# One encoder trunk on one core: bursts of small products, diagonal copies and early products put in another order

## The chip, the core and the metric

The kernel runs on one core of one Trainium2 chip. A core has a matrix engine (TensorE, PE in the profile, with its weight loads as PEld), three engines for element-wise work (VectorE or DVE, ScalarE or ACT, GpSimd or POOL) and a sync engine (SP) that mostly issues DMA transfers; ACT and POOL issue transfers too. Each engine runs its own instructions in its own order and waits on semaphores for the others. The metric is the device time of one execution in microseconds (us); a kernel's time is the median of its runs.

## The reference

The reference is a two-layer encoder over 1,024 tokens of width 1,024, with 16 learned tokens put in front (1,040 rows). Each layer:

```python
h = h + hybrid_mixer(rmsnorm(h, norm1_w[l]), w_in[l], conv_qkv_w[l], ...)
h = h + swiglu(rmsnorm(h, norm2_w[l]), w_gate_up[l], w_down[l])
```

The mixer projects to queries, keys and values of 4 heads of 128 channels, to gates, and to three inputs of a short convolution. Keys and queries are convolved and brought to unit length, and a gated delta rule is run over the sequence in both directions, in chunks. For each chunk and head it solves with a unit triangular matrix made from the products of the chunk's keys:

```python
M = jnp.where(strict, jnp.einsum('bnhid,bnhjd->bnhij', kb, k) * decay_mat, 0.0)
A = M + jnp.eye(CHUNK, dtype=M.dtype)
u = lax.linalg.triangular_solve(A, vb, left_side=True, lower=True, unit_diagonal=True)
```

The result is normalised, gated, joined with the convolution's output and projected back. The feed-forward part is `(silu(gate) * up) @ w_down` with 2,816 hidden channels. A last normalisation ends it.

## The kernel before

**Layout and precision.** Activations lie transposed: channels on the 128 partitions, the 1,040 positions along the free dimension, cut into three pieces of 346 to 348 columns (two of 512 in the second layer's last stages). Every dense product is made of three: an operand is split into a high part (a rounded copy made on ACT) and a low part (the remainder, made on DVE), and high x high, high x low and low x high are summed in PSUM (`dense`, L142, with its matmuls at L153 to L155, and `prod`, L1056, with L1061 to L1063). Each weight block is loaded by DMA, split by `wsplit` (ACT L126 for the high part, DVE L127 for the low one) or by `w_op` (L1043, L1044), and used by three matmuls per 128 rows of the contraction. Matmuls in plain float32, as the small ones below, leave two records each in the trace.

**Order.** The engines' order is not written out by hand. The program is traced in its order, each instruction carries a priority (`at_prio`, `low`), and a list scheduler with a simulated timeline orders every engine's instructions before the kernel runs. The function `after(ins, prev)` adds a dependency by hand. Work beside the dense products is put into three queues, `jobs`, `jobs2` and `jobs3`; after every piece of a dense product `dense` takes one entry off each (`None` is an empty turn). That way chunk work is spread over the projections.

**First layer's sums.** `first_sums` (L267) squares the eight input tiles, half on ACT and half on DVE, and sums each over the partitions with four 128x32 matmuls (L265), four column groups side by side.

**Chunk work.** With nine chunks of 128 positions (the first has 16), `chunk_p(c)` (L464) multiplies the chunk's keys with themselves (four matmuls, L474, in a PSUM bank "b" of two), fetches the decays, makes the exponentials (ACT L480) and writes the triangular matrices `Pv` of both directions (DVE L483). `k_out(c)` (L439) transposes the chunk's keys on PE (four transpositions, L445, in the one bank "a"), copies them on ACT (L447) and stores them. Before, `k_out` goes through `jobs` and `chunk_p` through `jobs2`, and both come up in the same pieces.

**Inverting the triangular matrices.** A 128x128 matrix is cut into 32x32 blocks. `sub_start` (L524) copies the diagonal blocks of each direction with four ACT copies (L535), turns them with a 32x32 transposition on DVE (L537) and loads unit matrices; `substitute(d)` (L540) then inverts the diagonal blocks on DVE, direction 0 first and direction 1 afterwards. `invert(d)` (L551) joins the blocks on PE: `first` (32x32 products, L574), `second_third` (32x32, L587 and L588) and five calls of `fourth_fifth` (64x64, L607 and L609) through `jobs3`. There are 32 matrices per direction (eight chunks times four heads), so `first` makes 64 small products and `second_third` 96, in two halves of 16 matrices each, with a PSUM bank for each half. Each call of `fourth_fifth` takes eight matrices; the fourth product of one group of eight runs beside the fifth of the group before it.

**Early products.** The feed-forward part uses a scheme with seven products of half matrices in place of eight. Its first four row blocks begin with two products each, made while the output projection still runs: `early_part(f, q)` (L1087) loads a weight block, splits it and calls `prod` for each bank (two in the first layer, one in the second).

Of the kernel before, what the change touches and what calls it, by code (L numbers as in the profile page):

```python
# [15 lines left out]
KT = 8  # L16
# [26 lines left out]
def trunk(ctx: ExitStack, tc: tile.TileContext, xT, w_in, w_ba, w_out, w_gu, w_dn,  # L43
# [12 lines left out]
    def big(tag, dt=F32):  # L56
        return sb.tile([128, 4, L], dt, tag=tag, name=nm(tag))
# [56 lines left out]
    mmp = [None]  # L114
    evp = [None]
    jobs, jobs2, jobs3 = [], [], []
    whi_done = [None]
    lov = [False]

    def wsplit(src, hi, lo, raw=None):  # L120

        kk = src.shape[1]
        if raw is None:
            raw = wp.tile([128, WK, 128], F32, tag="raw", bufs=2, name=nm("raw"))
        dma(raw[:, 0:kk, :], src)
        whi_done[0] = act(out=hi, in_=raw[:, 0:kk, :], func=AF.Copy)  # L126
        tt(out=lo, in0=raw[:, 0:kk, :], in1=hi.bitcast(F32), op=ALU.subtract)  # L127

    def wload(src, nk):

# [127 lines left out]

    def square(i, m):
        if m < 4:  # L260
            act(out=sqs[i], in_=hv[m], func=AF.Square)
        else:
            tt(out=sqs[i], in0=hv[m], in1=hv[m], op=ALU.mult)
        for j in range(4):
            mm(fps[32 * j:32 * j + 32, 0:260], ones[:, 0:32], sqs[i][:, 260 * j:260 * j + 260], start=(i == 0), stop=(i == KT - 1), skip_group_check=True)  # L265
# [30 lines left out]
    for l in range(DEPTH):  # L296
# [139 lines left out]
                qdma(bc, rnd[r + h].partition_broadcast(128))  # L436
                tt(out=dst[:, h, :], in0=dst[:, h, :], in1=bc, op=ALU.mult)

        def k_out(c):  # L439

            n = 16 if c == 0 else 128
            s0 = 0 if c == 0 else 16 + 128 * (c - 1)
            ps = pa()
            for h in range(H):
                nc.tensor.transpose(ps[0:n, h * 128:(h + 1) * 128], KTt[:, h, s0:s0 + n], ident)  # L445
# [18 lines left out]
        def chunk_p(c):  # L464
# [6 lines left out]
            n, s0 = span(c)  # L471
            kk = bank("b").rearrange("p (h i) -> p h i", h=4)
            for h in range(H):
                mm(kk[0:n, h, 0:n], KTt[:, h, s0:s0 + n], KTt[:, h, s0:s0 + n], start=True, stop=True)  # L474
# [46 lines left out]
        subs = {}  # L521
        Tm = None

        def sub_start():  # L524

            nonlocal Tm
            tmp0.append(big(Y[0][2]))
            Tm = sb.tile([128, 2, 128], F32, tag="off", name=nm("Tm")).rearrange("p a b -> p (a b)")
            v = [tmp0[0][:, i, 0:1024] for i in range(4)]
            for d in range(2):  # L530
                W, Xi = (v[0], v[2]) if d == 0 else [c4k("x")[:, 0:1024] for _ in range(2)]
                W, Xi, dg = (t.rearrange("p (a b) -> p a b", a=32) for t in (W, Xi, v[3 - 2 * d]))
                dma(Xi, eye_d)
                for b in range(4):
                    act(out=dg[B[b]], in_=Pv[d][B[b], :, B[b]], func=AF.Copy)  # L535

                nc.vector.transpose(out=W, in_=dg.rearrange("p q i -> p i q"))  # L537
                subs[d] = W, Xi

        def substitute(d):  # L540
            W, Xi = subs[d]
# [9 lines left out]
        def invert(d):  # L551
# [24 lines left out]
                    for (f, s) in pairs:  # L576
                        act(out=QS[B[s], qs, :], in_=ps[B[s]], func=AF.Copy, scale=-1.0)

            def second_third():
                f0, s0 = pairs[0]  # L580
                fo, so = 32 * (f0 % 2), 32 * (s0 % 2)
                for qs in halves:
                    ps = fb(32)

                    def turn(q):
                        for (f, s) in pairs:
                            mm(ps[B[f], q - qs.start, :], QS[B[s], q, :], P_[B[s], q, B[s]], start=True, stop=True, skip_group_check=True)  # L587
                        mm(ps[B[s0], q - qs.start, :], P_[B[s0], q, B[s0]], QS[B[s0], q, :], start=True, stop=True, skip_group_check=True)  # L588

                    low(lambda: [turn(q) for q in range(qs.start, qs.stop)])  # L590
                    for (f, s) in pairs:
                        act(out=P_[B[f], qs, B[s]], in_=ps[B[f]], func=AF.Copy)
                    act(out=X64[B[s0], qs, fo:fo + 32], in_=ps[B[s0]], func=AF.Copy)
                    nc.vector.tensor_copy(X64[B[f0], qs, fo:fo + 32], XB[B[f0], qs, :])
                    nc.vector.tensor_copy(X64[B[s0], qs, so:so + 32], XB[B[s0], qs, :])
                    nc.vector.memset(X64[B[f0], qs, so:so + 32], 0.0)


            F_, S_ = (slice(0, 64), slice(64, 128)) if d == 0 else (slice(64, 128), slice(0, 64))

            def fourth_fifth(q4, q5):

                ps = fb(64)

                def turn(q):
                    if q4 is not None:
                        mm(ps[S_, q, :], P_[F_, 8 * q4 + q, S_], X64[F_, 8 * q4 + q, :], start=True, stop=True, skip_group_check=True)  # L607
                    if q5 is not None:
                        mm(ps[F_, q, :], X64[S_, 8 * q5 + q, :], P_[S_, 8 * q5 + q, S_], start=True, stop=True, skip_group_check=True)  # L609

                low(lambda: [turn(q) for q in range(8)])
                if q4 is not None:
                    act(out=X64[S_, 8 * q4:8 * q4 + 8, :], in_=ps[S_], func=AF.Copy, scale=-1.0)
                if q5 is not None:
                    act(out=P_[F_, 8 * q5:8 * q5 + 8, S_], in_=ps[F_], func=AF.Copy)
# [437 lines left out]
        CW = E if E * 4 > 1024 else NB  # L1053
        NJ = NB // CW

        def prod(ps, w, t, j, first, stop=True):  # L1056
            nk = w[0].shape[1]
            for k in range(nk):
                cs = slice(CW * j, CW * j + CW)
                th, tl = (t[0][k], t[1][k]) if isinstance(t[0], list) else (t[0][:, k, :], t[1][:, k, :])  # L1060
                mm(ps[:, :CW], w[0][:, k, :], th[:, cs], start=first and k == 0, stop=False, skip_group_check=True)  # L1061
                mm(ps[:, :CW], w[0][:, k, :], tl[:, cs], start=False, stop=False, skip_group_check=True)  # L1062
                mm(ps[:, :CW], w[1][:, k, :], th[:, cs], start=False, stop=stop and k == nk - 1, skip_group_check=True)  # L1063

        def raw4(tag):
            if tag == "raw":
# [16 lines left out]

        NE = 4
        early, bks0 = {}, {}

        def early_part(f, q):  # L1087

# [536 lines left out]
```

## Time and profile before

| what | value |
|---|---|
| median of 3 runs | 2476.99 us |
| lowest and highest run | 2471.99 and 2478.96 us |
| the profiled execution | 2479.11 us |
| its span, first to last instruction | 2477.3 us |
| mean granted TensorE clock | 0.996 |
| DMA traffic | 335.26 MB, 135 GB/s |
| chain that ended last | PE 90%, DVE 4%, DMA 3%, ACT 2% |

The profile is of one execution. "Busy" is the time in which an engine's instructions were under way. Matmuls overlap in the pipeline and their ends are modelled, so a row's duration is longer than the distance to the next start; where distances matter, starts are compared. A timeline row gives the start and the length in us, the engine, the line, the operation, output and inputs, the shape and the count of merged instructions, and in brackets the idle time before it and who ended it. 32\*32, 64\*64 and 128\*32 are the rows and columns of the array that a matmul uses. The granted clock is TensorE's share of full speed.

### The profile page before, as it was taken

How to read it: one execution, taken by the hardware profiler on the slowest of the kernel's cores; microseconds unless marked ns; L12 is line 12 of the kernel's file. 1: busy time of each engine (PE TensorE's matmuls, PEld its weight loads, DVE VectorE, ACT ScalarE, POOL GpSimd, SP SyncE). 2: the span in 40 equal slices, each digit the busy share in tenths (PEclk: the TensorE clock that was granted, in tenths of full speed). 3: DMA queues.
4: the chain of work that ended last, by engine and by line, in shares of the span. 5: the costliest groups of instructions: out<-in, count | busy, mean ns of one | idle time of the engine just before them, and what ended most of it. 6: DMA issues, size and time to landing. Idle time of an engine off the chain costs nothing.

```text
span 2477.3 us, 44868 instructions
## 1 busy us (share of the span) xinstructions
PE 2450.6 (99%) x17530; PEld 2255.6 (91%) x17530; DVE 1778.2 (72%) x3296; ACT 1054.9 (43%) x1964; POOL 67.3 (3%) x157
## 2 busy tenths in 40 slices
PE   9999999999999999999999999999999999999998
PEld 8989999999999999999999888998978888888887
DVE  6888355769877777877657884456798777678774
ACT  6654333445333333444446543334553333334544
POOL 0120000000000000000001100000000000000002
PEclk9999999999999999999999999999999999999999
DMA  4545353534223332674224443445442233238641
GB/s 133 160 146 190 114 166 118 192 93 141 101 94 108 110 102 79 208 238 150 89 83 155 146 159 116 149 138 200 124 139 90 97 107 113 94 106 259 198 138 69
DMA packets 201321, 335.26 MB, mean 135 GB/s; under 512 B 23404, under 2 KB 88356, under 8 KB 201108
## 3 DMA queue, kind: packets, MB, share of 16 engines
q1 hardware_dynamic: 172996, 293.83, 36.9%
q10 hardware_dynamic: 25936, 34.19, 4.3%
q0 software_dynamic: 2176, 4.36, 0.6%
q8 instruction: 138, 2.26, 0.4%
q14 instruction: 75, 0.61, 0.1%
HBM read 250.31 MB, written 81.99 MB: 134 GB/s over the span
## 4 chain that ended last, share of the span: by engine, by line
PE 90%; DVE 4%; DMA 3%; ACT 2%; issue 1%; SPq 0%; ACTq 0%; DVEq 0%
PE pacc L155 10%; PE pacc L153 10%; PE pacc L154 10%; PE pacc L1063 4%; PE pacc L1061 4%; PE pacc L1062 4%; PE pb L1063 3%; PE pb L1061 3%; PE pb L1062 3%; PE pf L1063 3%; PE pf L1061 3%; PE pf L1062 3%; PE pacc L1484 2%; PE pacc L1481 2%; PE pacc L1483 2%; PE pa L1061 1%
## 5 line engine op out<-in xcount | busy, mean ns | idle before, releaser
L153 PE MATMUL pacc<-a,whi 128*128 128x346 f32 (+1 forms) x800 | 262.3, 328 | 1.5 <-ACT whi L126 1.0
L155 PE MATMUL pacc<-a,wlo 128*128 128x346 f32 (+1 forms) x800 | 261.1, 327 | 1.3 <-DVE wlo L127 1.2
L153 PE MATMUL pacc<-b,whi 128*128 128x346 f32 (+2 forms) x672 | 234.5, 349 | 0.6 <-ACT whi L126 0.6
L155 PE MATMUL pacc<-b,wlo 128*128 128x346 f32 (+2 forms) x672 | 233.7, 349 | 0.8 <-DVE wlo L127 0.8
L154 PE MATMUL pacc<-a,whi 128*128 128x346 f32 (+1 forms) x681 | 222.9, 328 | 1.3 <-DVE a L174 0.6
L154 PE MATMUL pacc<-b,whi 128*128 128x346 f32 (+2 forms) x580 | 200.8, 346 | 0.0
L126 ACT ACTIVATE whi<-raw 128x512 fp32r<-128x512 f32 x166 | 104.3, 631 | 218.3 <-PE pacc L154 158.2
L127 DVE TENSOR_TENSOR wlo<-raw,whi 128x512 fp32r<-128x512 f32 x166 | 113.6, 686 | 66.2 <-ACT whi L126 62.6
L155 PEld LDWEIGHTS pacc<-a,wlo 128*128 128x128 f32 x800 | 151.3, 189 | 4.0 <-DVE wlo L127 1.8
L153 PEld LDWEIGHTS pacc<-a,whi 128*128 128x128 f32 x800 | 151.2, 189 | 3.9 <-ACT whi L126 1.2
L153 PEld LDWEIGHTS pacc<-b,whi 128*128 128x128 f32 x672 | 127.2, 189 | 12.2 <-issue 1.9
L155 PEld LDWEIGHTS pacc<-b,wlo 128*128 128x128 f32 x672 | 126.9, 189 | 10.7 <-issue 1.3
L154 PEld LDWEIGHTS pacc<-a,whi 128*128 128x128 f32 x681 | 128.8, 189 | 5.0 <-DVE a L174 1.3
L1043 ACT ACTIVATE whi<-rw 128x512 fp32r<-128x512 f32 x92 | 57.9, 633 | 142.4 <-PE pf L1062 40.8
L154 PEld LDWEIGHTS pacc<-b,whi 128*128 128x128 f32 x580 | 109.8, 189 | 7.0 <-issue 0.4
L1043 ACT ACTIVATE b<-rw 128x512 fp32r<-128x512 f32 x64 | 40.1, 631 | 134.3 <-PE pacc L1062 42.1
L1043 ACT ACTIVATE a<-rw 128x512 fp32r<-128x512 f32 x64 | 40.3, 631 | 93.0 <-PE pacc L1062 60.0
L313 DVE TENSOR_TENSOR a<-pacc,rstd 128x346 f32<-128x346 f32 (+2 forms) x59 | 32.6, 554 | 59.7 <-PE pacc L155 59.4
L1044 DVE TENSOR_TENSOR wlo<-rw,whi 128x512 fp32r<-128x512 f32 x92 | 62.6, 684 | 3.4 <-ACT whi L1043 3.1
L313 DVE TENSOR_TENSOR b<-pacc,rstd 128x346 f32<-128x346 f32 (+1 forms) x63 | 32.2, 513 | 45.2 <-PE pacc L155 45.2
L1061 PE MATMUL pacc<-b,whi 128*128 128x260 f32 (+1 forms) x172 | 53.3, 310 | 0.2 <-ACT c L1097 0.2
L1062 PE MATMUL pacc<-b,whi 128*128 128x260 f32 (+1 forms) x172 | 53.3, 310 | 0.0
(981 smaller groups left out, 7863.6 us busy)
## 6 DMA issues: line engine op xcount, KB each, us to landing
raw<-in_w_in SPq DMA_DIRECT2D x110, 256.0 KB
raw<-in_w_gu SPq DMA_DIRECT2D x104, 256.0 KB
rw<-in_w_gu SPq DMA_DIRECT2D x88, 256.0 KB
rw<-in_w_dn SPq DMA_DIRECT2D x94, 192.0 KB
rec<-vkd SPq DMA_DIRECT2D x61, 256.0 KB
raw<-in_w_out SPq DMA_DIRECT2D x48, 256.0 KB
b<-ad SPq DMA_DIRECT2D x45, 260.0 KB
a<-ad SPq DMA_DIRECT2D x45, 256.0 KB
```

The lines of the kernel that those rows point to most:

```text
L126: whi_done[0] = act(out=hi, in_=raw[:, 0:kk, :], func=AF.Copy)
L127: tt(out=lo, in0=raw[:, 0:kk, :], in1=hi.bitcast(F32), op=ALU.subtract)
L153: mm(ps[:, :n], wh, xh[:, n0:n1], start=(k == 0), stop=False)
L154: mm(ps[:, :n], wh, xl[:, n0:n1], start=False, stop=False)
L155: mm(ps[:, :n], wl, xh[:, n0:n1], start=False, stop=(k == K - 1))
L313: tt(out=t[:, n0:n1], in0=ps, in1=rstd[:, n0:n1], op=ALU.mult)
L1043: act(out=hi, in_=src, func=AF.Copy)
L1044: tt(out=lo, in0=src, in1=hi.bitcast(F32), op=ALU.subtract)
L1061: mm(ps[:, :CW], w[0][:, k, :], th[:, cs], start=first and k == 0, stop=False, skip_group_check=True)
L1062: mm(ps[:, :CW], w[0][:, k, :], tl[:, cs], start=False, stop=False, skip_group_check=True)
L1063: mm(ps[:, :CW], w[1][:, k, :], th[:, cs], start=False, stop=stop and k == nk - 1, skip_group_check=True)
L1481: one = mm(ps[:, :CW], wh[:, k, :], th[:, cs], start=st, stop=False, skip_group_check=True)
```

## The change

Six edits, none of which changes what is computed:

1. `second_third` takes one half as an argument and becomes two entries of `jobs3` in place of one.
2. `fourth_fifth` takes lists: three calls in place of five. The first makes the fourth products of 16 matrices, the second those of the other 16 beside the fifth products of the first 16, the third the remaining fifth products.
3. `sub_start` takes a direction. Direction 0 is run at once as before. Direction 1 gives a list of five steps (four ACT copies, one DVE transposition), which go into `jobs3` during the v tiles, each ordered behind the latest weight split on its engine; its unit matrix is loaded then too.
4. `prod` takes the last matmul of the previous early product and puts its own first matmul behind it, so that the early products run in program order.
5. `first_sums` makes two squares and then their eight matmuls, the first of which waits for the second square.
6. `k_out(c)` leaves `jobs` and is called inside `chunk_p(c)`, with its first transposition behind the chunk's last key product.

The core of the diff:

```diff
-    whi_done = [None]
+    whi_done = [None, None]
...
-        tt(out=lo, in0=raw[:, 0:kk, :], in1=hi.bitcast(F32), op=ALU.subtract)
+        whi_done[1] = tt(out=lo, in0=raw[:, 0:kk, :], in1=hi.bitcast(F32), op=ALU.subtract)
...
     def first_sums():
-        for i, m in enumerate((0, 4, 1, 5, 2, 6, 3, 7)):
-            square(i, m)
+        order = (0, 4, 1, 5, 2, 6, 3, 7)
+        for i0 in (0, 2, 4, 6):
+            ready = [square(i, order[i]) for i in (i0, i0 + 1)]
+            for i in (i0, i0 + 1):
+                for j in range(4):
+                    one = mm(fps[32 * j:32 * j + 32, 0:260], ones[:, 0:32], sqs[i][:, 260 * j:260 * j + 260], start=(i == 0), stop=(i == KT - 1), skip_group_check=True)
+                    if i == i0 and j == 0:
+                        after(one, ready[1])
...
-        def k_out(c):
+        def k_out(c, prev):
...
-                nc.tensor.transpose(ps[0:n, h * 128:(h + 1) * 128], KTt[:, h, s0:s0 + n], ident)
+                after(nc.tensor.transpose(ps[0:n, h * 128:(h + 1) * 128], KTt[:, h, s0:s0 + n], ident), prev if h == 0 else None)
...
-                mm(kk[0:n, h, 0:n], KTt[:, h, s0:s0 + n], KTt[:, h, s0:s0 + n], start=True, stop=True)
+                end = mm(kk[0:n, h, 0:n], KTt[:, h, s0:s0 + n], KTt[:, h, s0:s0 + n], start=True, stop=True)
+            k_out(c, end)
...
-        def sub_start():
+        def sub_start(d):
...
+            dma(Xi, eye_d)
+            subs[d] = W, Xi
+            steps = [lambda b=b: after(act(out=dg[B[b]], in_=Pv[d][B[b], :, B[b]], func=AF.Copy), whi_done[0] if d else None) for b in range(4)]
+            return steps + [lambda: after(nc.vector.transpose(out=W, in_=dg.rearrange("p q i -> p i q")), whi_done[1] if d else None)]
...
-            def second_third():
+            def second_third(qs):
...
-            def fourth_fifth(q4, q5):
+            def fourth_fifth(q4s, q5s):
...
+                n = max(len(q4s), len(q5s))
+                pss = [fb(64) for _ in range(n)]
...
-            return [first, second_third] + [lambda a=a, b=b: fourth_fifth(a, b) for a, b in ((0, None), (1, 0), (2, 1), (3, 2), (None, 3))]
+            return [first] + [lambda qs=qs: second_third(qs) for qs in halves] + [lambda a=a, b=b: fourth_fifth(a, b) for a, b in (((0, 1), ()), ((2, 3), (0, 1)), ((), (2, 3)))]
...
-                jobs.append(None)
-                jobs.extend([lambda c=c: k_out(c) for c in range(9)])
...
-        sub_start()
+        for f in sub_start(0):
+            f()
...
+        st1 = sub_start(1)
+        jobs3.extend([None, None, None, st1[0], st1[1], None, st1[2], st1[3], st1[4]])
...
-        def prod(ps, w, t, j, first, stop=True):
+        def prod(ps, w, t, j, first, stop=True, prev=None):
...
+                one = mm(ps[:, :CW], w[0][:, k, :], th[:, cs], start=first and k == 0, stop=False, skip_group_check=True)
+                if prev is not None and k == 0:
+                    after(one, prev)
...
+            return one
...
-                prod(bks0[f][j], w, T[("B11", "B21")[q]], j, q == 0)
+                turn_e[0] = prod(bks0[f][j], w, T[("B11", "B21")[q]], j, q == 0, prev=turn_e[0])
```

More of the change, by code (lines that the diff above doesn't have):

```diff
@@ L260, in square @@
         if m < 4:
[L261 to L265, printed above, removed]
-    def first_sums():
-        for i, m in enumerate((0, 4, 1, 5, 2, 6, 3, 7)):
-            square(i, m)
+            return act(out=sqs[i], in_=hv[m], func=AF.Square)
+        return tt(out=sqs[i], in0=hv[m], in1=hv[m], op=ALU.mult)
+    def first_sums():
+        order = (0, 4, 1, 5, 2, 6, 3, 7)
[6 more added lines that the diff above has]
+                        after(one, ready[1])
         finish_bc(ss, 0, L, dram.tile([4, 260], F32, name=nm("rsd")), fps)
@@ L577, in first @@
                         act(out=QS[B[s], qs, :], in_=ps[B[s]], func=AF.Copy, scale=-1.0)
-            def second_third():
+            def second_third(qs):
                 f0, s0 = pairs[0]
                 fo, so = 32 * (f0 % 2), 32 * (s0 % 2)
[L582 to L590, printed above, removed]
-                    for (f, s) in pairs:
[L592 to L596, printed above, removed]
@@ L599, in invert @@
-            F_, S_ = (slice(0, 64), slice(64, 128)) if d == 0 else (slice(64, 128), slice(0, 64))
-            def fourth_fifth(q4, q5):
[L603 to L615, printed above, removed]
@@ L617, in invert, with turn @@
-            return [first, second_third] + [lambda a=a, b=b: fourth_fifth(a, b) for a, b in ((0, None), (1, 0), (2, 1), (3, 2), (None, 3))]
+                ps = fb(32)
+                def turn(q):
+                    for (f, s) in pairs:
+                        mm(ps[B[f], q - qs.start, :], QS[B[s], q, :], P_[B[s], q, B[s]], start=True, stop=True, skip_group_check=True)
+                    mm(ps[B[s0], q - qs.start, :], P_[B[s0], q, B[s0]], QS[B[s0], q, :], start=True, stop=True, skip_group_check=True)
@@ new lines, in second_third @@
+                low(lambda: [turn(q) for q in range(qs.start, qs.stop)])
+                for (f, s) in pairs:
+                    act(out=P_[B[f], qs, B[s]], in_=ps[B[f]], func=AF.Copy)
+                act(out=X64[B[s0], qs, fo:fo + 32], in_=ps[B[s0]], func=AF.Copy)
+                nc.vector.tensor_copy(X64[B[f0], qs, fo:fo + 32], XB[B[f0], qs, :])
+                nc.vector.tensor_copy(X64[B[s0], qs, so:so + 32], XB[B[s0], qs, :])
+                nc.vector.memset(X64[B[f0], qs, so:so + 32], 0.0)
@@ new lines, in invert, with turns @@
+            F_, S_ = (slice(0, 64), slice(64, 128)) if d == 0 else (slice(64, 128), slice(0, 64))
+            def fourth_fifth(q4s, q5s):
+                n = max(len(q4s), len(q5s))
+                pss = [fb(64) for _ in range(n)]
+                def turns(i):
+                    for q in range(8):
+                        if q4s:
+                            mm(pss[i][S_, q, :], P_[F_, 8 * q4s[i] + q, S_], X64[F_, 8 * q4s[i] + q, :], start=True, stop=True, skip_group_check=True)
+                        if q5s:
+                            mm(pss[i][F_, q, :], X64[S_, 8 * q5s[i] + q, :], P_[S_, 8 * q5s[i] + q, S_], start=True, stop=True, skip_group_check=True)
+                low(lambda: [turns(i) for i in range(n)])
+                for i, q4 in enumerate(q4s):
+                    act(out=X64[S_, 8 * q4:8 * q4 + 8, :], in_=pss[i][S_], func=AF.Copy, scale=-1.0)
+                for i, q5 in enumerate(q5s):
+                    act(out=P_[F_, 8 * q5:8 * q5 + 8, S_], in_=pss[i][F_], func=AF.Copy)
@@ L1085, in trunk @@
         early, bks0 = {}, {}
+        turn_e = [None]
         def early_part(f, q):
```

18 lines of the change are left out of this document (6 added, 12 removed).

## The prediction

> **What bounds the kernel now.** I read the head of the page first, then the list of TensorE's waits, then the stretches around the longest of them, and last the order of single instructions there.
>
> ```profile
> span 2477.3 us, 44868 instructions
> ## 1 busy us (share of the span) xinstructions
> PE 2450.6 (99%) x17530; PEld 2255.6 (91%) x17530; DVE 1778.2 (72%) x3296; ACT 1054.9 (43%) x1964; POOL 67.3 (3%) x157
> ```
>
> TensorE (PE) is busy for 99% of the span, so its idle time, 2477.3 - 2450.6 = 26.7 us, and what it runs slowly or needlessly are all that can be won. A microsecond taken out of PE is a microsecond of the total, because no other engine comes near. Where it idles, by who ended the wait (total, times, longest):
>
> ```profile
> PE pf L587 <- issue: 2.5, 2, 2.1
> PE pb L1061 <- ACT whi L1043: 2.0, 1, 2.0
> PE pacc L155 <- DVE wlo L127: 2.0, 2, 1.2
> PE pb L587 <- issue: 1.9, 1, 1.9
> PE pacc L153 <- ACT whi L126: 1.6, 2, 1.0
> PE pa L230 <- DVE sel L282: 1.1, 1, 1.1
> PE pb L474 <- DVE P L483: 1.0, 3, 0.7
> ```
>
> Six of these seven stand at steps that the change rearranges. Two of them end with no semaphore at all ("issue"): they stand in the middle of the 32x32 products of line 587. The stretches around three of the waits (length, busy time of PE, weight loads, DVE, ACT and POOL with counts, granted clock, DMA share, GB/s):
>
> ```profile
> 1450.70:1452.70 2.00, 0.00 (x0) 0.00 (x0) 1.83 (x6) 0.90 (x2) 0.00 (x0) 1.00 0.37 119
> 1452.70:1456.20 3.50, 3.48 (x22) 2.93 (x23) 1.89 (x5) 2.36 (x4) 0.00 (x0) 0.51 0.02 5
> 1818.50:1820.60 2.10, 0.12 (x1) 0.00 (x0) 2.10 (x6) 2.10 (x4) 0.00 (x0) 1.00 0.35 116
> 1820.60:1825.00 4.40, 4.35 (x12) 3.33 (x13) 4.40 (x6) 2.24 (x4) 0.00 (x0) 0.61 0.31 88
> 1521.00:1523.10 2.10, 0.21 (x21) 0.10 (x12) 0.75 (x1) 1.81 (x4) 0.00 (x0) 1.00 0.50 184
> 1523.10:1528.00 4.90, 4.90 (x30) 3.91 (x31) 0.00 (x0) 1.77 (x3) 0.00 (x0) 0.65 0.22 85
> ```
>
> Each gap of about 2 us is followed by a stretch at a clock of 0.51 to 0.65. That second loss, (1 - clock) x length, is 3.5 x 0.49 = 1.7, 4.4 x 0.39 = 1.7 and 4.9 x 0.35 = 1.7 us, nearly as much as the gap, and counts as busy. The queues during the first gap:
>
> ```profile
> q8 instruction: 1, 0.02, 2.2%
> ```
>
> So one instruction transfer ran while PE stood without a wait. My reading: a burst of 96 small products (192 records and as many weight loads) eats instructions faster than they arrive.
>
> **The change part by part.**
>
> *A, half bursts* (second_third per half). The two line-587 rows idle 2.5 + 1.9 = 4.4 us, and two half-clock stretches cost 1.7 each: 7.8 us. With 24 dense products between the halves the supply can catch up. Against it stand four more changes of form, whose price is read from the 64x64 groups:
>
> ```profile
> 1458.11 1.14 PE L607 MATMUL pf<-a,P 64*64 64x64 f32 x16
> 1459.18 0.42 PE L153 MATMUL pacc<-b,whi 128*128 128x348 f32 x1
> 1459.44 0.32 PE L154 MATMUL pacc<-b,whi 128*128 128x348 f32 x1
> 1459.61 0.32 PE L155 MATMUL pacc<-b,wlo 128*128 128x348 f32 x1
> 1459.85 0.33 PE L607 MATMUL pf<-a,P 64*64 64x64 f32 x2
> 1460.11 0.42 PE L153 MATMUL pacc<-b,whi 128*128 128x348 f32 x1
> ```
>
> From start to start: two neighbouring dense products are 0.16 to 0.17 apart; into the small form it is 0.24 (0.08 more), after the first dense product behind it 0.26 (0.10 more). The group of 16 records takes 1.07, the piece of 2 takes 0.26, so one product (2 records) costs (1.07 - 0.26) / 7 = 0.116, and a change of form 0.26 - 0.116 + 0.18 = 0.32. Four more cost 1.3. A = -7.8 + 1.3 = -6.5; ends -6.5 and +1.3 (the pauses stay).
>
> [...]
>
> *E, 64x64 groups, three for five.* In the middle groups both kinds of product run in turn:
>
> ```profile
> 1463.44 0.27 PE L609 MATMUL pf<-P,a 64*64 64x64 f32 x1
> ...
> 1464.52 0.55 PE L744 MATMUL pa<-ident,a3f 128*128 128x128 f32 x3
> ```
>
> 1464.52 - 1463.44 = 1.08 for 32 records, what 16 of one kind take: a second kind is free. Before, each direction has five groups of 1.07 + 0.18 = 1.25, so 6.25. After, it has 16 turns of one kind, 16 paired and 16 of one kind: 48 x 0.116 + 3 x 0.32 = 6.53. Over four directions that is +1.1, less 0.44 for each stray piece like that at 1459.85 that no longer splits off. E = +0.7, with that one piece credited; ends -0.7 (four pieces) and +1.1. So this part loses by its own arithmetic, as fewer pairings outweigh fewer changes.
>
> [...]
>
> *B, spread diagonal copies.* Eight copies of line 535 follow each other on ACT, then two 32x32 transpositions on DVE:
>
> ```profile
> L535 ACT ACTIVATE b<-P x8: 1041/1056/1062, 143.2 to 150.7; 32x1024 f32<-32x1024 f32 x8
> ```
>
> ```profile
> 152.02 2.02 DVE L537 STREAM_TRANSPOSE x<-b 128x1024 f32<-128x1024 f32 x1
> ...
> 154.14 1.28 DVE L127 TENSOR_TENSOR wlo<-raw,whi 128x512 fp32r<-128x512 f32 x2
> ```
>
> The weights' high split waits behind the copies, the low split behind the transposition; these are the rows L153 and L155 of the wait list, 1.6 + 2.0 = 3.6 us in two layers. With direction 1's share moved into nine chunks of the v tiles, ACT is free after four copies, 143.2 + 4.2 = 147.4, well before the last began at 150.7. The new dependencies are on ACT's and DVE's own earlier splits: they order and do not stop an engine. Moved along are the load of the unit matrix on SP's queue (once a layer, now behind direction 0's substitution) and the allocation of two buffers; direction 1's substitution starts only when direction 0's is done, which covers both. If that cover were gone, substitution would start late, but its products are low in the order and dense ones stand before them. ACT is 43% busy, so a copy of 1.06 may now and then push a split: B = -3.2; ends -3.6 and 0.
>
> *C, ordered early products.* In layer 1 (PE, then DVE):
>
> ```profile
> 1818.23 0.39 PE L1063 MATMUL pacc<-a,wlo 128*128 128x512 f32 x1
> 1820.65 0.50 PE L1061 MATMUL pb<-a,whi 128*128 128x512 f32 x1 [2.03 <-ACT whi L1043]
> 1820.99 0.39 PE L1062 MATMUL pb<-a,whi 128*128 128x512 f32 x1
> 1821.21 0.52 PE L1061 MATMUL pacc<-b,whi 128*128 128x512 f32 x1
> ```
>
> ```profile
> 1819.16 0.68 DVE L1044 TENSOR_TENSOR wlo<-raw,whi 128x512 fp32r<-128x512 f32 x1
> ...
> 1822.69 0.68 DVE L1044 TENSOR_TENSOR wlo<-raw,whi 128x512 fp32r<-128x512 f32 x1
> ```
>
> Two products of a later part (pb<-a) were put ahead of the part that was ready (pacc<-b), and PE waited for the later part's weights. In order, PE does two products from 1818.46 on (0.23 each), waits for the low split until 1819.84 (0.9), runs ten to 1822.2, does two and waits for the next low split until 1823.37 (0.7). Instead of 2.0 + 1.7 (clock) that is 1.6: C = -2.1. What is late next is that low split. Ends: -3.7 (nothing waits), and +1.5, if in six parts the order takes away cover of one 0.23 product. Layer 0 counts as nothing: its parts wait for splits that are late in either order.
>
> *D, first sums in pairs.* A run of 4 records beside one of 16:
>
> ```profile
> 28.84 0.63 PE L265 MATMUL pb<-b,ones 128*32 128x260 f32 x4
> ```
>
> ```profile
> 1364.63 1.08 PE L626 MATMUL pf<-sq,sel 128*32 128x260 f32 x16
> ```
>
> Joining two saves 2 x 0.63 - 1.08 = 0.18, and 0.18 of entry and exit; four joins 1.4 at most, but neighbours were partly joined already: D = -0.6. The first product of a pair now waits on PE for DVE's square, with dense products behind it; at the list's longest wait on DVE, 1.2, four such cost +4.8. The squares' waits are under 1.0 and not in the list, so I stay near the low end.
>
> *F, key transpositions behind key products.* Each k_out keeps its chunk, but four transpositions now follow the chunk's products instead of preceding them:
>
> ```profile
> 1362.15 0.60 PE L445 MATMUL pa<-ident,a 128*128 128x128 f32 x4
> ```
>
> Their copy and store on ACT's queue go along. The three waits of L474 (1.0 in all) may vanish (-1.0) or each lose 0.60 of cover (+1.8). F = +0.4, the middle.
>
> Sum: -6.5 + 0.7 - 3.2 - 2.1 - 0.6 + 0.4 = -11.3. The profiled execution took 2479.11 (span 2477.3 and 1.8 around it), 2.1 above the median 2476.99; I take the difference from the median: **2465.7**.
>
> **Rivals.**
>
> *1, the pauses stay.* The instruction supply is late whatever the burst's length, or both halves run back to back because the first was not ready in its chunk. For it: the first products of a direction are a burst too. Against: only the longest bursts pause. A becomes +1.3: -11.3 + 7.8 = -3.5, 2473.5. [...]
>
> *2, the waits for weights move.* The splits are late elsewhere, as ACT and DVE do the same work. For it: DVE's 72%, and chains like 1819.16 to 1822.69. Against: PE has spare dense products among the v tiles. B and C become 0: -11.3 + 5.3 = -6.0, 2471.0.
>
> *3, slower: key products and transpositions stall together.* Each of the 18 chunk steps waits 0.7, as L474's worst, for DVE to free its bank, and has lost the 0.60 of transpositions as cover: 18 x 1.3 = 23.4, so +12.1, 2489.1. It decides from 11.3 / 1.3, nine steps, on; from fifteen it is slower by over 7.4 us. For it: those waits exist. Against: 3 of 18 steps had one.
>
> **How the numbers follow.** Forecast 0.66, rival 1 0.13, rival 2 0.14, rival 3 0.07. A measurement of this kernel tells about 0.3%, 7.4 us, from no change, so the line is at 2469.6: the forecast is faster, rivals 1 and 2 are within it, rival 3 is taken as slower. All good ends give -6.5 - 0.7 - 3.6 - 3.7 - 1.4 - 1.0 = -16.9, 2460.1; the runs before spread from 2471.99 to 2478.96, so I add 3 below, and 2.5 above rival 1: 2457 to 2476. Rival 3 is left out.
>
> **What would show it.** Right: no "issue" wait at the 32x32 products and no clock under 0.7 behind them; no wait of L153/L155 near the diagonal copies; parts of the early products one after the other, with waits under 1 us; twelve 64x64 groups of 2.0 us. Wrong: an idle stretch of 2 us that lowers the clock at any new place, since each brings 1.7 more; waits of L474 in many chunks.

## The result, and the profile after

| kernel | median, us | runs | ratio to before (95% interval) |
|---|---|---|---|
| before | 2477.58 (2471.99 to 2479.76) | 16 | 1 |
| after | 2469.29 (2465.50 to 2473.65) | 16 | 0.9971 (0.9965 to 0.9978) |

The change makes the kernel faster by 8.3 us by the medians and by 7.2 us (0.0029 x 2477.58) by the ratio. The forecast was -11.3 us: the interval of the ratio, -5.5 to -8.7 us, leaves it out, and 2469.29 lies nearer to rival 2's 2471.0 than to the forecast's 2465.7. The profiled execution after took 2473.65 us, the top of its sixteen runs, so what its trace shows is a little worse than the median.

The head of the page after:

```profile
span 2471.9 us, 44873 instructions
...
PE 2448.0 (99%) x17530; PEld 2259.7 (91%) x17530; DVE 1779.7 (72%) x3296; ACT 1057.9 (43%) x1964; POOL 67.2 (3%) x157
```

The span is 5.4 us shorter. Idle went from 26.7 to 2471.9 - 2448.0 = 23.9 us, and busy time fell by 2.6 us. Little of that is clock won back: ahead of the last 15 us both profiles have four stretches of half clock of 3.41 us each, before at 510.66, 1452.74, 1524.42 and 1821.38 us, after at 10.74, 58.53, 481.78 and 1454.58 us. What else makes up the 2.6 us was not worked out. TensorE's waits after (total, times, longest):

```profile
PE pf L610 <- ACT b L616: 1.9, 1, 1.9
PE pf L588 <- issue: 1.8, 1, 1.8
PE pb L477 <- DVE P L487: 1.5, 1, 1.5
...
PE pacc L1065 <- ACT b L1105: 0.7, 1, 0.7
PE pf L589 <- issue: 0.7, 1, 0.7
PE pf L1065 <- ACT b L1105: 0.7, 1, 0.7
...
PE pacc L153 <- ACT whi L126: 0.2, 1, 0.2
```

Of the five rows the forecast counted on, three are gone or small: the low split (L155, 2.0 before), the high split (L153, 1.6 before, 0.2 now) and the early products' weight (2.0 before; now waits of 0.7 for copies). The "issue" waits, 4.4 before, are still 2.5. New is the first row. The stretches around them, a burst of 32x32 products to a row first (length, busy PE, PEld, DVE, ACT, POOL with counts, granted clock, DMA share, GB/s):

```profile
278.24:279.38 1.14, 1.14 (x98) 1.10 (x97) 0.52 (x1) 0.00 (x0) 0.00 (x0) 1.00 0.00 0
283.40:284.54 1.14, 1.14 (x98) 1.10 (x97) 1.03 (x2) 1.07 (x2) 0.00 (x0) 1.00 0.52 172
1450.85:1455.17 4.32, 2.56 (x193) 2.38 (x193) 4.15 (x13) 1.62 (x2) 0.00 (x0) 0.93 0.56 161
```

```profile
1452.84:1454.60 1.76, 0.00 (x1) 0.00 (x1) 1.73 (x6) 1.06 (x1) 0.00 (x0) 0.99 0.37 107
1454.60:1458.10 3.50, 3.50 (x36) 3.44 (x37) 3.36 (x9) 3.40 (x6) 0.00 (x0) 0.52 0.84 250
222.14:224.05 1.91, 0.00 (x0) 0.00 (x0) 0.64 (x2) 1.27 (x3) 0.00 (x0) 1.00 0.20 62
224.05:227.55 3.50, 3.50 (x73) 3.43 (x74) 3.43 (x9) 2.76 (x5) 0.00 (x0) 1.00 0.57 195
```

Direction 1 (first two rows) runs as 96 + 96 records, 1.14 us each, with no gap. Direction 0 (third row) still has 192 records in one stretch, stands idle for 1.76 us in it, and then runs 3.5 us at a clock of 0.52. The idle 1.91 us at 222.14, just as long, is followed by full clock. So a gap doesn't always bring the second loss.

That gap's cause lies in ACT's queue (SPq and ACTq rows are DMA issues):

```profile
217.03 0.60 ACT L747 ACTIVATE b3f<-pa 128x512 f32<-128x512 f32 x1
217.66 0.38 ACTq L748 DMA_DIRECT2D vkd<-b3f  x1
222.37 0.34 ACTq L516 DMA_DIRECT2D dt<-dtd  x1
222.75 0.63 ACT L126 ACTIVATE whi<-raw 128x512 fp32r<-128x512 f32 x1 [5.13 <-DMA aqd<-dt]
223.01 0.33 ACTq L516 DMA_DIRECT2D dt<-dtd  x1
223.41 1.08 ACT L616 ACTIVATE b<-pf 64x512 f32<-64x512 f32 x2
```

ACT did nothing for 5.13 us, because a load (L516) waited for its buffer; a weight split and the copies L616 that the next 64x64 group needs stood behind it.

### The profile page after: what moved, and what is told of

It reads as the page before. It is cut to its first block, busy times and chain, and to the rows that moved or that the text cites. A ratio compares the mean times of both kernels' runs of the same rounds, so it can differ in the third digit from the quotient of the medians.

```text
span 2471.9 us, 44873 instructions
## 1 busy us (share of the span) xinstructions
PE 2448.0 (99%) x17530; PEld 2259.7 (91%) x17530; DVE 1779.7 (72%) x3296; ACT 1057.9 (43%) x1964; POOL 67.2 (3%) x157
## 4 chain that ended last, share of the span: by engine, by line
PE 92%; DVE 4%; DMA 2%; ACT 1%; issue 1%; SPq 0%; ACTq 0%; DVEq 0%
PE pacc L153 10%; PE pacc L154 10%; PE pacc L155 10%; PE pacc L1069 4%; PE pacc L1065 4%; PE pacc L1068 4%; PE pb L1065 3%; PE pb L1069 3%; PE pb L1068 3%; PE pf L1065 3%; PE pf L1069 3%; PE pf L1068 3%; PE pacc L1492 2%; PE pacc L1489 2%; PE pacc L1491 2%; PE pa L1065 1%
## 5 line engine op out<-in xcount | busy, mean ns | idle before, releaser
L153 PE MATMUL pacc<-a,whi 128*128 128x346 f32 (+1 forms) x800 | 263.0, 329 | 2.3 <-ACT a L950 1.0
L155 PE MATMUL pacc<-a,wlo 128*128 128x346 f32 (+1 forms) x800 | 261.0, 327 | 0.1
L153 PE MATMUL pacc<-b,whi 128*128 128x346 f32 (+2 forms) x672 | 233.7, 348 | 0.0
L155 PE MATMUL pacc<-b,wlo 128*128 128x346 f32 (+2 forms) x672 | 232.1, 347 | 0.0
L153 PEld LDWEIGHTS pacc<-a,whi 128*128 128x128 f32 x800 | 151.8, 190 | 5.8 <-ACT a L950 1.8
L155 PEld LDWEIGHTS pacc<-a,wlo 128*128 128x128 f32 x800 | 151.8, 190 | 1.7 <-issue 1.0
L153 PEld LDWEIGHTS pacc<-b,whi 128*128 128x128 f32 x672 | 126.8, 189 | 10.3 <-issue 1.9
L155 PEld LDWEIGHTS pacc<-b,wlo 128*128 128x128 f32 x672 | 126.5, 189 | 9.2 <-issue 1.3
L1065 PE MATMUL pacc<-b,whi 128*128 128x260 f32 (+1 forms) x172 | 52.7, 307 | 0.7 <-ACT b L1105 0.7
L1069 PE MATMUL pacc<-b,wlo 128*128 128x260 f32 (+1 forms) x172 | 52.7, 306 | 0.0
```

The source lines that it names most:

```text
L153: mm(ps[:, :n], wh, xh[:, n0:n1], start=(k == 0), stop=False)
L155: mm(ps[:, :n], wl, xh[:, n0:n1], start=False, stop=(k == K - 1))
L1065: one = mm(ps[:, :CW], w[0][:, k, :], th[:, cs], start=first and k == 0, stop=False, skip_group_check=True)
L1069: one = mm(ps[:, :CW], w[1][:, k, :], th[:, cs], start=False, stop=stop and k == nk - 1, skip_group_check=True)
```

## The experiments

Unless said otherwise an experiment starts from the changed kernel. The twelve kernels were timed in three sets of four, each set on another chip and beside the kernel before (medians 2475.46, 2475.84 and 2477.89 us); kernels of different sets are compared by their ratios to it.

**Halves only.** Before, with edit 1 alone:

```diff
-            def second_third():
+            def second_third(qs):
...
-            return [first, second_third] + [...]
+            return [first] + [lambda qs=qs: second_third(qs) for qs in halves] + [...]
```

> The kernel before with the 32x32 products of a direction in two separate steps, and nothing else of the change. Theory (the halves only help where 64 or so dense records stand between them; direction 0's first half becomes ready too late in both layers, so both halves still run as one burst of 192 records): direction 1 runs as 96 + 96 records with no pause, direction 0 as one burst with a pause in layer 0 or layer 1; the time falls by 2 to 4 us against before. Rival a, the prediction's own term (all pauses go): -6.5 us. Rival b (the pauses have nothing to do with the length of the burst): the same two or three pauses inside line 583's products, +1.3 us.

Measured 0.9997 (0.9987 to 1.0006), -0.7 us. Direction 1's halves are apart and without a gap, direction 0's are one burst of 192. (In the profile after 53 and 52 records lie between direction 1's halves, where the expectation says 64 or so.) In layer 1 its gap is as long as before, but look at the clock behind it:

```profile
1447.89:1449.78 1.89, 0.00 (x2) 0.00 (x1) 1.72 (x6) 0.89 (x2) 0.00 (x0) 1.00 0.37 122
1449.78:1453.28 3.50, 3.50 (x24) 2.98 (x25) 3.26 (x9) 2.64 (x5) 0.00 (x0) 1.00 0.02 5
```

The interval excludes -6.5 us, the full term A, and reaches to -3.2 us at most; the 2 to 4 us expected here are not borne out either. New waits of 1.2 and 0.8 us in this trace (early products, scan) may have eaten part of the gain; which part isn't shown.

**Half a block of instructions more.** Before, with 32 small warm-up products, unused, at the start:

```diff
+    for _ in range(32):
+        mm(pw[:, 0:16], ones, ones[:, 0:16], start=True, stop=True)
```

> The kernel before with 32 more small warm-up products (128x16, output not used) at its start: 128 more TensorE instructions, half a block of 256, and nothing else. They add 32 x 0.05 to 0.1 us at most, while TensorE waits for the first loads anyway. Theory (a pause stands where the queue runs dry at the 193rd instruction of a block of 256, if the 300 instructions ahead of it ran in under 3.7 us): the pauses leave their products; in before they stood at instruction 3265, 23745 and 25281 of TensorE's stream, which are now 3393, 23873 and 25409, the middle of a block. Burst 2 of layer 0 (17.99 to 19.49 blocks before, 18.49 to 19.99 now) gets one at 4929 + 128 or so, where block position x.75 = 19.75 falls into it late; the bursts of layer 1 (92.0 to 93.5 and 98.0 to 99.5 before) get theirs at another record or none. Rival (the data or the banks of these products make them wait): the pauses stand at the same products as before, 2.3 and 2.1 us in layer 1.

Counting TensorE's records from the first (matmuls, weight loads and sequencer instructions), the longest gap between two starts inside each burst of 192 stands here:

| burst | before | with 128 records more |
|---|---|---|
| layer 0, direction 0 | 0.59 us at 3265 | none |
| layer 0, direction 1 | none | 1.72 us at 5057 |
| layer 1, direction 0 | 2.27 us at 23745 | none |
| layer 1, direction 1 | 2.08 us at 25281 | none |

Every one of the four numbers leaves 193 when divided by 256. The products are the same, yet three gaps vanished and one appeared, at the record named in advance. The 3.7 us for 300 instructions, in the next expectation the time of a fetch, is an estimate from the three gaps of layer 1, which end 3.85 and 3.66 us (before) and 3.53 us (after) from the start of the record 300 places earlier. The two of layer 0 end at 3.01 (before) and 4.74 us (after), so the figure is rough; at the same place of every other block of the two profiles it is 5.59 us or more. The rows, two undisturbed bursts and the new gap:

```profile
1461.36:1463.51 2.15, 2.15 (x193) 2.11 (x192) 1.92 (x6) 1.15 (x3) 0.00 (x0) 1.00 0.33 89
1529.31:1531.46 2.15, 2.15 (x193) 2.11 (x192) 1.51 (x3) 1.80 (x3) 0.00 (x0) 1.00 0.15 51
285.33:286.85 1.52, 0.00 (x0) 0.00 (x0) 0.00 (x0) 1.14 (x2) 0.00 (x0) 1.00 0.00 0
286.85:290.35 3.50, 3.50 (x40) 3.44 (x41) 0.00 (x0) 1.77 (x3) 0.00 (x0) 0.52 0.02 5
```

So the gaps belong to the instruction stream, not to data or banks. One more appeared outside the four bursts, 1.2 us in a 64x64 group at 221.82 us, at the same place of a block. The queue of instruction transfers bears the block out; before and in the profile after its row is

```profile
q8 instruction: 138, 2.26, 0.4%
```

which for the 35,328 records of TensorE before is 256 records a transfer. The whole was slower, 1.0034 (1.0020 to 1.0049), which was not expected: the first sums began at 40.82 us in place of 24.60, so the start lost more than the bursts won. The added products themselves took that time:

```profile
5.92 13.67 PE L232 MATMUL pa<-ones 128*128 128x16 f32 x64
```

Each of their 64 records took 0.21 us, so a product of two records 0.42, where 0.05 to 0.1 had been allowed for. Behind them the dense products stood 0.29 us apart until 24.2 us, in place of 0.16. What made the small ones so slow isn't shown.

**A wait between the halves.**

```diff
+                        if q == qs.start and f == f0:
+                            after(one, lastd[0])
```

> The changed kernel, where the first 32x32 product of each half also waits on TensorE for the last dense product issued ahead of it in the program, so that the two halves of direction 0 can't close up. Theory (a burst of 192 records outruns the supply of instructions, one of 96 does not, since 300 instructions then take longer than the 3.7 us in which the next block of 256 is fetched): four bursts of 96 records in every layer, no idle stretch inside them, no clock near 0.50 at 1454 to 1458; 0.7 (layer 0's pause) + 1.8 (layer 1's) + 1.7 (half clock) = 4.2 us less than the changed kernel, minus two more changes of form at 0.32: -3.5 us, and a ratio to before of about 0.9957. Rival (the supply is late at these places whatever the length): pauses of 0.7 to 2 us stay inside a half burst; 0 to +1 us against the changed kernel. Rival (the wait itself costs): the second half then holds up dense products in the order, a wait of 1 us or more at the half's first product.

`lastd[0]` is the last dense product emitted before. Measured 0.9972 (0.9961 to 0.9983): no gain over the change. The order of TensorE's instructions came out exactly as in the changed kernel, since direction 0's first half becomes ready so late that the dense product tied to the second half is done by then as well. The run serves as a second sample of the change: it has 192 records in direction 0, with gaps of 0.3 and 1.6 us, but not the wait of 1.9 us at a 64x64 group.

**Direction 0 eight pieces later.**

```diff
-                jobs3.extend(invert(0))
+                jobs3.extend([None] * 8 + invert(0))
```

> The changed kernel, where direction 0's steps (first 32x32 products, two halves, three groups) begin eight chunks later in the list of work between the dense chunks, and nothing else. Compiled order: in the changed kernel direction 0's two halves stand side by side in both layers (192 records), because its substitution is late and all its steps with it; eight chunks later the halves of both directions stand 28 or 24 dense products apart. Theory (a burst of 192 records outruns the instruction supply, one of 96 can't): eight bursts of 96 records, none with an idle stretch inside; the 0.7 of layer 0 and, in layer 1, the 1.8 idle and the 1.7 of half clock behind it go, for two more changes of form of 0.32 each: -3.6 us against the changed kernel, ratio to before about 0.9956. Rival (supply late at these places whatever the length): idle stretches of 0.7 to 2 us remain in the halves or move to the 64x64 groups, no gain. Rival (what comes later is itself late): new waits of TensorE of 1 us or more behind 1500 us, where direction 1 begins at once after direction 0; 0 to +3 us.

The order of direction 0 in layer 1, small products and the larger ones between them (`dense` in this list counts transpositions too):

```
before     first 64, dense 27, second/third 96
after      first 64, dense 28, second/third 96
e9_late    first 64, dense 28, second/third 48, dense 28, second/third 48
```

Measured 0.9954 (0.9942 to 0.9967), where 0.9956 was expected. All four bursts of direction 0 run without a gap:

```profile
218.01:219.15 1.14, 1.14 (x97) 1.10 (x97) 1.14 (x3) 0.00 (x0) 0.00 (x0) 1.00 0.99 397
224.06:225.20 1.14, 1.14 (x98) 1.10 (x97) 1.14 (x4) 0.00 (x0) 0.00 (x0) 1.00 0.69 187
1462.15:1463.29 1.14, 1.14 (x98) 1.10 (x97) 1.07 (x3) 0.85 (x2) 0.00 (x0) 1.00 1.05 397
1468.21:1469.35 1.14, 1.14 (x98) 1.10 (x97) 1.10 (x3) 0.00 (x0) 0.00 (x0) 1.00 0.85 320
```

No wait ends with "issue" any more, and what is left at the top of its list is work that the change doesn't touch or has tied together:

```profile
PE pb L1065 <- ACT a L1105: 1.6, 1, 1.6
PE pb L477 <- DVE P L487: 1.2, 1, 1.2
PE pa L230 <- DVE sel L285: 1.1, 1, 1.1
```

**Diagonal copies only.** Before, with edit 3 alone:

```diff
+        st1 = sub_start(1)
+        jobs3.extend([None, None, None, st1[0], st1[1], None, st1[2], st1[3], st1[4]])
```

> The kernel before with direction 1's four diagonal copies and its transposition spread over nine chunks, and nothing else of the change. Theory (the prediction's B): the waits of L155 for the low split (2.0 us in two layers) and of L153 for the high split (1.6 us) go: -3.2 us, ratio about 0.9987. Rival 2 of the prediction (the splits are late elsewhere): other waits of 0.5 to 1 us on whi or wlo near the v tiles, -1 to 0 us.

Measured 0.9988 (0.9979 to 0.9997): -3.0 us for a forecast of -3.2. The waits of L155 and L153 for the splits are out of its list; the top of it is what the other edits are about:

```profile
PE pb L1062 <- ACT whi L1044: 2.4, 1, 2.4
PE pf L585 <- issue: 2.1, 1, 2.1
PE pb L585 <- issue: 1.8, 1, 1.8
```

**Early order only.** Before, with edit 4 alone:

```diff
+                if prev is not None and k == 0:
+                    after(one, prev)
```

> The kernel before with the early products in order, and nothing else of the change. Theory: the wait of 2.0 us at 1818.5 and the stretch at a clock of 0.61 behind it (1.7 us) go, waits of 0.4 to 0.9 us for copies take their place: -2.1 us by the prediction, up to -3.8 by the traces of after (3.05 to 1.3 us of excess in layer 0, 4.56 to 2.4 us in layer 1). Rival (the order only moves the wait): a wait of 1.5 us or more at another early product, with a low clock behind it, 0 us.

Measured 0.9998 (0.9989 to 1.0007). By the time alone -2.1 us is not excluded; the trace shows what the rival named. The wait for the weight is gone, and one of 2.73 us, with half clock behind it, stands at another product:

```profile
1814.97 0.40 PE L1065 MATMUL pacc<-a,wlo 128*128 128x512 f32 x1
1815.06 1.99 ACT L1010 ACTIVATE P<-b 128x1024 fp32r<-128x1024 f32 x2
...
1816.95 0.61 ACT L1043 ACTIVATE whi<-raw 128x512 fp32r<-128x512 f32 x1
...
1817.47 0.58 ACT L1101 ACTIVATE b<-pacc 128x512 f32<-128x512 f32 x1
...
1818.10 0.68 PE L1061 MATMUL pacc<-b,whi 128*128 128x512 f32 x1 [2.73 <-ACT b L1101]
```

The bank pacc is full after the product at 1814.97. Its copy L1101 stands on ACT behind two copies of another tile (L1010, 1.99 us) and a weight's split, so the next product into pacc starts at 1818.10. In order, the second product of a row block needs the bank that the first has just filled; out of order, the next block's product, into another bank, covered that copy.

**Five groups.** Edit 2 undone:

```diff
-            def fourth_fifth(q4s, q5s):
+            def fourth_fifth(q4, q5):
```

> The changed kernel with five groups of 64x64 products of eight turns each, as before, in place of three of sixteen. By the prediction's arithmetic three groups cost +0.7 us in all (6.53 for 6.25 us a direction, less the pieces that split off), and the wait of 1.9 us of L610 for the copy of L616 is a new one on top. Theory: 0.3 x 4 less in the groups, and the 1.9 us wait at 221.8 is gone, since a group needs one bank that the copies have to free, not two: -2 to -3 us against the changed kernel. [...] Rival (the 1.9 us wait comes from the load that stands in ACT's queue and not from the groups): the same wait at another product near 222 us, and no more than 1.2 us less.

Measured 0.9987 (0.9977 to 0.9996), about 4 us slower than the change by the ratios where 2 to 3 us of gain were expected, though its groups take the time computed for them (1.07 and 1.08 us) and the 1.9 us wait has become one of 0.6. Its trace loses time elsewhere: 2.2 us at the early products, for the same bank's copy as above. That doesn't account for the 4 us, since the profiled run (2470.03 us) was faster than the kernel's median (2472.57) and than the profiled run of the change. So I tried it again beside the kernel with direction 0 late.

**Late, four ways.** The late kernel once more; with five groups; with the first sums as before (edit 5 undone); with the early order as before (edit 4 undone). The edits are the ones shown, the third being

```diff
-            ready = [square(i, order[i]) for i in (i0, i0 + 1)]
...
+        for i, m in enumerate((0, 4, 1, 5, 2, 6, 3, 7)):
+            square(i, m)
```

> The kernel e9_late once more, as the common base for the three others of this call, and to see how far two profiles of one kernel differ in where they wait. Expected: ratio to before 0.9954 again, within its interval 0.9942 to 0.9967; no idle stretch inside the bursts of 96 records; the wait near 600 to 1030 us or 1795 to 1825 us for a copy that empties a bank of the early products (1.6 us at pb in the first profile) may stand at another product or be gone.

> e9_late with five groups of 64x64 products in place of three. The groups that were built in: three of 2.005, 2.012 and 2.005 us are 6.02 a direction, five of 1.07 and 1.08 are 5.38; each group adds 0.18 for entry and exit. Theory (the prediction's E): five are 6.28 and three 6.56, so five are faster by 0.28 a direction, 1.1 us in four, less 0.44 for each of three stray pieces of one product in layer 1 and layer 0: -0.2 to -1.1 us against e9_late. [...]

> e9_late with the first sums as before the change (each square with its own four products). The prediction had -0.6 us for the pairs; the traces show the same groups of 18, 10, 4, 8 and 24 records with and without. Theory: 0 us, same groups, start of the first sums at 24.5 to 25.4 us in either. Rival (the pairs hold up the start, as the changed kernel's profile had its first sums at 26.78 in place of 24.60): 1 to 2 us faster than e9_late.

> e9_late with the early products in the order of before. Theory (the order only trades the wait for a weight for the wait for the copy that empties a bank, as the change alone gave 0.9998): 0 to +1 us against e9_late; its profile has a wait of about 2 us of L1061 for ACT's whi at 1795 to 1825 us in place of waits of 1 to 1.6 us for the bank's copy. Rival, the prediction's C: +2.1 us.

| kernel | median, us | ratio to before |
|---|---|---|
| late, again | 2466.00 | 0.9954 (0.9941 to 0.9967) |
| late, five groups | 2464.11 | 0.9951 (0.9936 to 0.9966) |
| late, first sums back | 2466.14 | 0.9954 (0.9940 to 0.9969) |
| late, early order back | 2464.29 | 0.9950 (0.9936 to 0.9965) |

None differs from the late kernel: the means of the five runs are 2465.8, 2465.1, 2466.2 and 2465.0 us, with an uncertainty of some 2.5 us on a difference. The number of groups, the pairs of sums and the early order are each worth nothing that five runs can tell, and the 4 us of the run before is not repeated. With the early order undone the wait for the weight near 1800 us was expected to come back at 2 us; it is 0.7 us, so its length hangs on what else the schedule holds. The first sums start at 24.54 and 25.02 us in the two profiles of the late kernel and at 24.64 with the pairs undone, so the pairs didn't delay them. The 26.78 of the profile after, and 27.10 in the late kernel with five groups, stand in the only two profiles that have a stretch of half clock at 10.7 to 14.3 us.

**Key transpositions back.** Edit 6 undone:

```diff
+                jobs.extend([lambda c=c: k_out(c) for c in range(9)])
...
-            k_out(c, end)
```

> The changed kernel with the key transpositions taken back to their own step in the list, ahead of the key products' chunks. The prediction has +0.4 us for tying them to the products. The traces of before and after read -1 us: before, waits of 0.9 us in layer 0 and 1.8 us in layer 1 near the key products, after it one of 1.5 us in layer 0 alone (L477 for DVE's P). Theory: +1 us against the changed kernel, the waits of L474 in two or three chunks come back and the one of 1.5 us goes. Rival (the tie costs, since the wait of 1.5 to 1.9 us stands in every trace with it): -0.5 to -1.5 us.

Measured 0.9981 (0.9972 to 0.9990), 2.5 us slower than the change, with intervals that overlap. The waits at the key products in layer 0 of the changed kernel, and in layer 1 of this one:

```profile
PE pb L477 <- DVE P L487: 1.5, 1, 1.5
PE pa L448 <- ACT kt L450: 0.4, 1, 0.4
```

```profile
PE pb L477 <- DVE P L486: 0.8, 2, 0.5
```

The wait of 0.4 us stands in layer 0 of both. So the tie takes away 0.8 us in layer 1 and brings one wait of 1.5 us in layer 0: by these rows it costs 0.7 us, where the times say that it gains 2.5. Of the 1.8 us that the expectation counts in layer 1 before, 0.8 are L155's wait for the low split, which is edit 3's. What edit 6 is worth stays open.

## Why the prediction was right, step by step

The side and the range held; the size came out a third smaller, 7.2 us for 11.3. The parts:

| part | forecast, us | measured, us | from |
|---|---|---|---|
| A, half bursts | -6.5 | -0.7 | edit 1 alone |
| A with direction 0 apart too | -6.5 | -4.9 | -0.7 and 0.9954 against 0.9971 |
| B, diagonal copies | -3.2 | -3.0 | edit 3 alone |
| C, early order | -2.1 | -0.5 | edit 4 alone; undone in the late kernel: no difference |
| D, first sums | -0.6 | 0 | undone in the late kernel |
| E, groups | +0.7 | 0 | undone in the late kernel |
| F, transpositions | +0.4 | -2.5 (not told from 0) | undone in the changed kernel |

Each comes with 2 to 4 us of uncertainty, so the sum of -6.7 (with A at -0.7) agrees with -7.2 without proving it.

*A.* The mechanism, an instruction supply that a long burst outruns, is borne out by the shifted kernel (128 records more took three gaps away and brought one of 1.72 us), and by the late one that halves cure it where they stand apart (four bursts of 1.14 us, no gap). The step that failed is "with 24 dense products between the halves the supply can catch up": it holds in direction 1 alone. In direction 0 the rival's second condition came true: the first half was not ready in its turn, and both ran back to back. In the profile after, A is one "issue" wait of 1.9 and one stretch at half clock (1.7) less, and two changes of form (0.64) more: -3.0. The forecast's -11.3 us is reached by the late kernel: (1 - 0.9954) x 2475.84 = 11.4. That the two agree to 0.1 us is luck: by the table A and C fall 1.6 us short each even there, and F gives 2.9 us more than forecast.

*The second loss.* "Each brings 1.7 more" was too much. In the fourteen profiles TensorE stood idle for 1.15 us or longer 35 times behind the first 20 us; a stretch at half clock followed 14 times: 7 of 8 gaps of 2 us or more, 6 of 18 between 1.4 and 2, 1 of 9 below. The stretch is always 3.41 us long, so 1.7 us is right as a size but not as a certainty. For gaps between 1.4 and 2 us, a third of it is the better term. And the second loss isn't tied to these gaps: in the same profiles, between 20 and 2440 us, 14 more such stretches follow no gap of 1.15 us or more, those of the profile after at 58.53 and 481.78 us among them. What brings these is not shown; with them the profile after has no fewer stretches than the profile before.

*B* held in mechanism and size. *C* named the wrong next-late step: it expected the low split, and the copy that empties the bank came first. The wait there took the place of the one removed, so C came out near 0 as rival 2 says, but not for its reason (late splits); rival 2's other half, B at 0, fell. (C's upper end, six times 0.23 us, is 1.4 and not 1.5; no other number rests on it.) *E*: a group of 16 turns takes 2.0 us, as computed; a loss of 0.7 us can't be told from none, while a gain of 2.6 us, eight groups fewer at 0.32 for a change of form, was not seen. *D*: the records stand in the same groups of 18, 10, 4 and 8 before and after, so there was no piece to join, and the -0.6 had no ground. *F* and rival 3: one long wait of 0.9 to 2.5 us at one chunk in layer 0, in every trace with the tie, not the fifteen stalls that would make it slower. (Without the tie, the shifted kernel has one of 1.7 us too, in layer 1.)

## What to carry to other kernels

Splitting a step helped here only where the halves ended up apart (0.9971 with direction 0's back to back, 0.9954 with them apart): look at the order that comes out, and where it is made by priorities, move the whole step to where its inputs are ready (0.9954) instead of adding a wait (0.9972). Before pricing an order of products, ask for each bank who empties it and what stands ahead of that copy on its engine (here two copies, 1.99 us, and a split, 0.61, for a wait of 2.73 us). A burst of 192 tiny records had a price that depended on its place in the instruction stream, from no gap to one of 2.27 us, so a change of a hundred instructions far ahead can move it, as the 128 records of the shifted kernel did.

## What the runs showed of the hardware

In the fourteen profiles every gap without a wait inside a run of small products, twenty in all, stood at the 192nd or 193rd record of a block of 256, one of them in a group of 64x64 products; none of the 60 bursts of 96 records had a gap inside. By the packet times kept in the traces TensorE went on 2.27 to 2.82 us after the latest transfer on the instruction queue had begun, in all twenty: I read that as the supply ending the gap. The block is the trace's own, 35,328 records in 138 transfers of 16,384 bytes before, and a crossing cost up to 2.3 us.

The same gap, at the same products, is followed by half clock in one run and by full clock in another (1.76 us: 0.52; 1.89 us: 1.00). Each half-clock stretch is 3.41 us long, and those of the profile before begin 942.08, 71.68 and 296.96 us apart, 276, 21 and 87 times 3.413 us; in the profile after it is 47.79, 423.25 and 972.80 us, 14, 124 and 285 times. Counted in such periods, the 1.76 us lay in one, but for its last 0.02 us, and the 1.89 us was cut into 1.31 and 0.58; the 1.91 us at 222.14 in the profile after, followed by full clock, was cut into 0.23 and 1.68. That the borders decide is my reading. In the fourteen profiles all eight periods with over 1.87 us of idle time were followed by half clock, and 7 of the 16 with 1.4 to 1.87 us; what brought the rest is not shown. By length alone, gaps of 1.15 to 2 us were followed by half clock 7 times of 27. Here is one of 2.06 us in the late kernel, where the tie's wait cost twice:

```profile
126.16:128.22 2.06, 0.00 (x0) 0.03 (x1) 2.06 (x6) 1.15 (x3) 0.00 (x0) 1.00 0.99 382
128.22:131.72 3.50, 3.50 (x19) 3.50 (x20) 3.50 (x11) 3.15 (x5) 0.00 (x0) 0.69 0.64 215
```
